# An earlier place for the first store's first transfer, coarser pieces in the first and the last tile, and the last store in two halves, in a SiLU-gate kernel

## The chip, the cores and the metric

One core of a Trainium2 chip. The metric is device time in microseconds (us) of the whole program, the median of several runs. The profile's span is some 2 us shorter than that time. All runs here are with a granted clock of 1.0.

## The reference

```python
def setup_inputs():
    batch, seq, dim = (32, 512, 2048)
    return {'x': np.random.randn(batch, seq, dim).astype(np.float32)}

def reference(x):
    half_dim = x.shape[-1] // 2
    x1, x2 = (x[..., :half_dim].copy(), x[..., half_dim:].copy())
    silu_x1 = x1 * (1 / (1 + np.exp(-x1)))
    return (silu_x1 * x2).astype(np.float32)
```

16,384 rows of 2,048 floats come in and rows of 1,024 go out: 134.2 MB read and 67.1 MB written, with one activation and one multiplication per output element.

## The kernel before

The rows are cut into 16 tiles. A tile gives each of the 128 partitions 8 rows, so it is an 8 MB load and a 4 MB store. Two input and two output buffers alternate. SyncE issues the loads. ScalarE (ACT) computes the SiLU and issues the stores. VectorE (DVE) multiplies in place.

```python
    K = 8
    KC_EDGE = 2
    OPENING = [                                   # (partitions, rows) of the first tile's four transfers
        (slice(0, None, 4), slice(0, 2)),         # 32 partitions x 2 rows: 256 KB
        (slice(0, None, 4), slice(2, None)),      # the same partitions, 6 rows: 768 KB
        (slice(2, None, 4), slice(None)),         # 32 partitions, 8 rows: 1 MB
        (slice(1, None, 2), slice(None)),         # 64 partitions, 8 rows: 2 MB
    ]
    # ... pools, views; silu() is one nc.scalar.activation, mul() one nc.vector.tensor_mul ...
    load(0)
    load(1)
    for i in range(n_tiles):
        xt = loaded.pop(i)
        ov = view(out_flat, i)
        ot = out_pool.tile([P, K, half], dt, name="ot")
        if i < n_tiles - 1:
            kc = KC_EDGE if i == 0 else K
            for c in range(0, K, kc):
                silu(ot, xt, c, c + kc)
                mul(ot, xt, c, c + kc)
            for ps, ks in OPENING if i == 0 else [(slice(None), slice(None))]:
                nc.scalar.dma_start(out=ov[ps, ks], in_=ot[ps, ks])
            if i + 2 < n_tiles:
                load(i + 2)
            continue
        cuts = list(range(0, K, KC_EDGE))         # the last tile: four pieces of 2 rows
        for n, c in enumerate(cuts + [None, None]):
            if c is not None:
                silu(ot, xt, c, c + KC_EDGE)
                mul(ot, xt, c, c + KC_EDGE)
            if n >= 2:
                b = cuts[n - 2]
                nc.scalar.dma_start(out=ov[:, b:b + KC_EDGE, :], in_=ot[:, b:b + KC_EDGE, :])
```

Of the kernel before, what the change touches and what calls it, by code (L numbers as in the profile page):

```python
# [1 line left out]

# [4 lines left out]


def issue_ahead_of_the_first_barrier(nc):




    head, body = nc.main_func.blocks[:2]
    load = next(ins for ins in body.instructions if type(ins).__name__ == "InstDMACopy")
    at = next(
        j for j, ins in enumerate(head.instructions)
        if ins.engine == load.engine and type(ins).__name__ == "InstDrain"
    )
    body.instructions = [ins for ins in body.instructions if ins.name != load.name]  # L20
    head.instructions = head.instructions[:at] + [load] + head.instructions[at:]


@with_exitstack
def kernel(
    ctx: ExitStack,
    tc: tile.TileContext,
    x: bass.AP,
    out: bass.AP,
):  # L30






    nc = tc.nc
    P = nc.NUM_PARTITIONS

    x_flat = x.flatten_outer_dims()  # L40
    out_flat = out.flatten_outer_dims()
    num_rows, in_cols = x_flat.shape
    half = in_cols // 2
    dt = x_flat.dtype

    K = 8
    KC_EDGE = 2
    OPENING = [
        (slice(0, None, 4), slice(0, 2)),
        (slice(0, None, 4), slice(2, None)),  # L50
        (slice(2, None, 4), slice(None)),
        (slice(1, None, 2), slice(None)),
    ]
    PLAN = [K] * (num_rows // (P * K))

    in_pool = ctx.enter_context(tc.tile_pool(name="in_pool", bufs=2))
    out_pool = ctx.enter_context(tc.tile_pool(name="out_pool", bufs=2))

    plan = []
    row = 0  # L60
    for k in PLAN:
        plan.append((row, k))
        row += P * k
    assert row == num_rows
    n_tiles = len(plan)

    def view(flat, i):
        row0, k = plan[i]
        return flat[row0:row0 + P * k].rearrange("(p k) d -> p k d", k=k)

    nc.at_finalize(issue_ahead_of_the_first_barrier)


    ctx.enter_context(tc.manual_schedule())

    loaded = {}

    def load(i):
        xt = in_pool.tile([P, K, in_cols], dt, name="xt")
        nc.sync.dma_start(out=xt[:, :plan[i][1], :], in_=view(x_flat, i))  # L80
        loaded[i] = xt

    def silu(ot, xt, c, ce):
        nc.scalar.activation(  # L84
            out=ot[:, c:ce, :],
            in_=xt[:, c:ce, :half],
            func=mybir.ActivationFunctionType.Silu,
        )

    def mul(ot, xt, c, ce):  # L90
        nc.vector.tensor_mul(  # L91
            out=ot[:, c:ce, :],
            in0=ot[:, c:ce, :],
            in1=xt[:, c:ce, half:],
# [6 lines that stand above are left out]
        ov = view(out_flat, i)  # L101
        ot = out_pool.tile([P, K, half], dt, name="ot")
        if i < n_tiles - 1:
            kc = KC_EDGE if i == 0 else K
            for c in range(0, K, kc):
                silu(ot, xt, c, c + kc)
                mul(ot, xt, c, c + kc)

            for ps, ks in OPENING if i == 0 else [(slice(None), slice(None))]:
                nc.scalar.dma_start(out=ov[ps, ks], in_=ot[ps, ks])  # L110
            if i + 2 < n_tiles:
                load(i + 2)
            continue

        cuts = list(range(0, K, KC_EDGE))
        for n, c in enumerate(cuts + [None, None]):
            if c is not None:
                silu(ot, xt, c, c + KC_EDGE)
                mul(ot, xt, c, c + KC_EDGE)
            if n >= 2:  # L120
                b = cuts[n - 2]
                nc.scalar.dma_start(out=ov[:, b:b + KC_EDGE, :], in_=ot[:, b:b + KC_EDGE, :])


# [1 line left out]
_INS = ['x']  # L126
_OUTS = [((32, 512, 1024), 'float32')]


# [23 lines left out]
```

## Time and profile before

| | before |
|---|---|
| median time (3 runs) | 470.49 us (470.48 to 470.6) |
| span | 468.5 us |
| ACT and DVE busy | 24% and 30% of the span |
| DMA | 430 GB/s over the span |

The page and its edges are read in the prediction. One more view: the windows of the kernel before. The columns are the stretch, its length, the busy time of DVE, ACT and POOL, the clock, the DMA share and GB/s.

```profile
36.00:44.00 8.00, 0.00 (x0) 0.00 (x0) 0.00 (x0) 1.00 1.21 492
26.00:48.00 22.00, 6.72 (x4) 6.85 (x3) 0.00 (x0) 1.00 1.03 429
```

A window books a packet whole where it starts, so the share can exceed 1 and 8 us are too short for a rate. The same windows of two kernels can still be held against each other.

A finer measure comes from the trace's packet records, and I call it **lost DMA time**: the length of a stretch, minus the time that the work done in it takes at the packets' undisturbed durations, as a mean over the 16 DMA engines. It counts both standing still and slow packets. The undisturbed pitch is 2.42 us for a 64 KB load packet and 1.21, 0.91, 0.61 and 0.31 us for store packets of 32, 24, 16 and 8 KB. For the kernel before it is 0.76 us from 26 to 48 us, and 0.0 to 0.02 us in every later stretch I tabulated. (Neighbouring packet records overlap by some 0.2% in the steady stretches. With their recorded durations taken as they are, the figure for a stretch of 22 us comes out about 0.05 us lower.) A "lane" below is one engine's string of packets. The records do not name the engine, so lanes are rebuilt from starts and ends.

### The profile page before, as it was taken

How to read it: one execution, taken by the hardware profiler on the slowest of the kernel's cores; microseconds unless marked ns; L12 is line 12 of the kernel's file. 1: busy time of each engine (PE TensorE's matmuls, PEld its weight loads, DVE VectorE, ACT ScalarE, POOL GpSimd, SP SyncE). 2: the span in 40 equal slices, each digit the busy share in tenths (PEclk: the TensorE clock that was granted, in tenths of full speed). 3: DMA queues.
4: the chain of work that ended last, by engine and by line, in shares of the span. 5: the costliest groups of instructions: out<-in, count | busy, mean ns of one | idle time of the engine just before them, and what ended most of it. 6: DMA issues, size and time to landing. Idle time of an engine off the chain costs nothing.

```text
span 468.5 us, 188 instructions
## 1 busy us (share of the span) xinstructions
DVE 139.5 (30%) x22; ACT 114.3 (24%) x23; POOL 0.2 (0%) x4
## 2 busy tenths in 40 slices
DVE  0070613407033070430704207052060510606151
ACT  1142306041060500505005050140601406023060
POOL 0000000000000000000000000000000000000000
DMA  9999999999999999999999999999999999999988
GB/s 431 392 453 380 448 425 425 492 403 403 448 476 420 403 448 425 470 403 428 422 492 403 403 448 487 408 403 448 425 470 403 425 425 492 403 403 448 481 371 357
DMA packets 5121, 201.34 MB, mean 430 GB/s; under 512 B 608, under 2 KB 608, under 8 KB 608
## 3 DMA queue, kind: packets, MB, share of 16 engines
q1 hardware_dynamic: 2304, 134.22, 66.4%
q10 hardware_dynamic: 2816, 67.11, 33.2%
q14 instruction: 1, 0.01, 0.0%
HBM read 134.22 MB, written 67.11 MB: 430 GB/s over the span
## 4 chain that ended last, share of the span: by engine, by line
DMA 72%; DVE 14%; ACT 11%; DVEq 0%; issue 0%; ACTq 0%
DMA xt<-in_x_dram 72%; DVE ot L91 14%; ACT ot L84 11%; DVEq L148 0%; ACTq L84 0%
## 5 line engine op out<-in xcount | busy, mean ns | idle before, releaser
L91 DVE TENSOR_TENSOR ot<-ot,xt 128x8192 f32<-128x8192 f32 (+1 forms) x22 | 139.5, 6362 | 319.6 <-ACT ot L84 319.6
L84 ACT ACTIVATE ot<-xt 128x8192 f32<-128x8192 f32 (+1 forms) x22 | 113.0, 5163 | 340.5 <-DMA xt<-in_x_dram 340.5
L84 ACT ACT_TABLE_LOAD x1 | 1.3, 1283 | 0.8 <-PEq L137 0.8
L137 POOL MEMSET const-bfloat16-1.0<- 128x1 bf16 x1 | 0.1, 101 | 0.0
L137 POOL MEMSET const-uint8-127<- 128x1 uint8 x1 | 0.1, 101 | 0.0
L137 POOL MEMSET const-float32-0.0<- 128x1 f32 x1 | 0.1, 98 | 0.2 <-issue 0.2
L137 POOL MEMSET const-float32-1.0<- 128x1 f32 x1 | 0.1, 98 | 0.0
## 6 DMA issues: line engine op xcount, KB each, us to landing
out_dram<-ot ACTq DMA_DIRECT2D x14, 4096.0 KB, 42.0
out_dram<-ot ACTq DMA_DIRECT2D x5, 1024.0 KB, 8.2
out_dram<-ot ACTq DMA_DIRECT2D x1, 2048.0 KB, 37.0
out_dram<-ot ACTq DMA_DIRECT2D x1, 768.0 KB, 11.7
xt<-in_x_dram SPq DMA_DIRECT2D x16, 42.1
out_dram<-ot ACTq DMA_DIRECT2D x1, 256.0 KB, 10.9
```

Source lines behind the costliest of these rows:

```text
L84: nc.scalar.activation(out=ot[:, c:ce, :], in_=xt[:, c:ce, :half], func=mybir.ActivationFunctionType.Silu,)
L91: nc.vector.tensor_mul(out=ot[:, c:ce, :], in0=ot[:, c:ce, :], in1=xt[:, c:ce, half:],)
L137: nc = _bacc.Bacc("TRN2", target_bir_lowering=False, num_devices=1)
```

## The change

The intent is to have the first store under way early, and to have fewer and larger pieces at the end. The first tile is computed in pieces of 2, 2 and 4 rows and the first transfer is issued after the second activation. The last tile is computed as 2, 2 and 4 rows and stored as two halves of 4.

```diff
-    KC_EDGE = 2
+    CHUNKS_FIRST = [2, 2, 4]
+    CHUNKS_LAST = [2, 2, 4]
+    KS = 4
@@ all tiles but the last
-            kc = KC_EDGE if i == 0 else K
-            for c in range(0, K, kc):
+            c = 0
+            chunks = CHUNKS_FIRST if i == 0 else [K]
+            parts = list(OPENING) if i == 0 else [(slice(None), slice(None))]
+            for n, kc in enumerate(chunks):
                 silu(ot, xt, c, c + kc)
+                if n == 1:
+                    ps, ks = parts.pop(0)
+                    nc.scalar.dma_start(out=ov[ps, ks], in_=ot[ps, ks])
                 mul(ot, xt, c, c + kc)
-            for ps, ks in OPENING if i == 0 else [(slice(None), slice(None))]:
+                c += kc
+            for ps, ks in parts:
                 nc.scalar.dma_start(out=ov[ps, ks], in_=ot[ps, ks])
@@ the last tile
-        cuts = list(range(0, K, KC_EDGE))
-        ... (four pieces, each stored two pieces later)
+        issued = None
+        c = 0
+        for kc in CHUNKS_LAST:
+            silu(ot, xt, c, c + kc)
+            if issued is None and c >= KS:
+                issued = slice(0, KS)
+                nc.scalar.dma_start(out=ov[:, issued], in_=ot[:, issued])
+            mul(ot, xt, c, c + kc)
+            c += kc
+        nc.scalar.dma_start(out=ov[:, KS:], in_=ot[:, KS:])
```

More of the change, by code (lines that the diff above doesn't have):

```diff
@@ L113 @@
             continue
-        cuts = list(range(0, K, KC_EDGE))
-        for n, c in enumerate(cuts + [None, None]):
-            if c is not None:
-                silu(ot, xt, c, c + KC_EDGE)
-                mul(ot, xt, c, c + KC_EDGE)
-            if n >= 2:
-                b = cuts[n - 2]
-                nc.scalar.dma_start(out=ov[:, b:b + KC_EDGE, :], in_=ot[:, b:b + KC_EDGE, :])
+        issued = None
[8 more added lines that the diff above has]
+        nc.scalar.dma_start(out=ov[:, KS:], in_=ot[:, KS:])
 _INS = ['x']
```

## The prediction

> **What bounds the kernel now.** I read the page first, then the windows (busy time and DMA by stretch), the timeline of the two edges, the waits, and last the trace's single DMA packet records, because the change touches only the first and the last tile.
>
> The page: compute is far from full, the DMA engines are full in all 40 slices but the last two, and those are at eight tenths.
>
> ```profile
> span 468.5 us, 188 instructions
> DVE 139.5 (30%) x22; ACT 114.3 (24%) x23; POOL 0.2 (0%) x4
> ...
> DMA  9999999999999999999999999999999999999988
> ...
> HBM read 134.22 MB, written 67.11 MB: 430 GB/s over the span
> ```
>
> The reader should see 201.3 MB in 468.5 us. Nothing in the change alters the bytes, so it can only win time in which DMA engines stand still or run slowly. The windows over five stretches and the tail say how much there is of that:
>
> ```profile
> 5.00:26.00 21.00, 2.18 (x1) 4.12 (x3) 0.00 (x0) 1.00 0.98 424
> 26.00:44.00 18.00, 6.72 (x4) 3.19 (x2) 0.00 (x0) 1.00 1.05 437
> 44.00:447.00 403.00, 121.69 (x14) 98.41 (x14) 0.00 (x0) 1.00 1.00 432
> 447.00:457.00 10.00, 6.80 (x4) 7.31 (x4) 0.00 (x0) 1.00 0.99 426
> 457.00:467.00 10.00, 2.10 (x1) 0.00 (x0) 0.00 (x0) 1.00 0.98 414
> ```
>
> The last two columns are the DMA share and GB/s. A window books a packet where it starts, so short windows are rough (1.05), but no stretch from 5 to 467 us has a hole worth a microsecond. The last row runs 4% under the middle one: there the packets are 8 KB instead of 32 KB.
>
> The packet records sharpen this. I spread each packet's bytes over its own duration and strung packets into 16 lanes, each beginning as another ends (the records do not name the engine, so the lanes are my reconstruction). From 1.0 us to 467.1 us the lanes have no gap to speak of: 0.07 us per lane in total. A 64 KB load packet takes 2.418 us, a 32 KB store packet 1.213 us, an 8 KB store packet 0.309 us. Slow packets occur in three places only, in us per lane: 0.73 at the very first load packets, 0.17 around 28 to 31 us, 0.57 in the load packet of 36.3 to 39.5 us (3.0 instead of 2.42 us in all lanes). Check: 16 tiles x 8 x 2.418 = 309.5; 15 store tiles x 8 x 1.213 = 145.6; the last tile 32 x 0.309 = 9.9; slow packets 1.5; sum 466.5 plus the start at 1.0 = 467.5, against a last packet ending at 467.13 (rounding and slight overlap). The remaining 1.4 us of the span is its end after the last packet.
>
> The edges in the timeline:
>
> ```profile
> 21.88 5.51 ACT L84 ACTIVATE ot<-xt 128x2048 f32<-128x2048 f32 x3 [19.83 <-DMA xt<-in_x_dram]
> 23.82 8.90 DVE L91 TENSOR_TENSOR ot<-ot,xt 128x2048 f32<-128x2048 f32 x4 [23.82 <-ACT ot L84]
> 26.15 0.55 ACTq L110 DMA_DIRECT2D out_dram<-ot  x1
> 27.30 1.89 ACT L84 ACTIVATE ot<-xt 128x2048 f32<-128x2048 f32 x1
> 32.75 1.78 ACTq L110 DMA_DIRECT2D out_dram<-ot  x3
> ...
> 450.20 8.90 DVE L91 TENSOR_TENSOR ot<-ot,xt 128x2048 f32<-128x2048 f32 x4 [15.17 <-ACT ot L84]
> 452.53 0.34 ACTq L122 DMA_DIRECT2D out_dram<-ot  x1
> 453.68 1.89 ACT L84 ACTIVATE ot<-xt 128x2048 f32<-128x2048 f32 x1
> 454.73 4.74 ACTq L122 DMA_DIRECT2D out_dram<-ot  x3
> ```
>
> Two things to see. The first transfer stands after all four activations in the code, yet goes out at 26.15 us, before the fourth activation starts: it waits for the first multiplication alone. And the chain of waits shows loads and compute alternating (72% DMA, 14% DVE, 11% ACT), but that chain is the longest dependency, not the limit: while ACT waits up to 22 us for a load, the engines carrying that load never stop.
>
> **What the Trainium skill says.** "Perfetto Trace Analysis", Roofline, puts a lone trn2 core's ceiling at its 16 DMA engines, about 435 GB/s; the spread packets run at 434 here, so it agrees. The same page, Per-instruction lifecycle, says that an activation's semaphore wait takes place in a queue behind the sequencer, which is then free for the next instruction; the 26.15 us issue agrees. "DMA: Bandwidth & Descriptors", Anatomy of one DMA, says that a DMA's wait happens on the issuing sequencer before dispatch: so an activation behind such an issue is held. Nothing here stands behind one, so this trace does not show it yet. The same page, Queues, rings and completion order, has each DMA engine take turns between queues by packets; the lanes alternate load, store, load, store wherever both queues have work.
>
> **The change part by part.**
>
> *First transfer issued between activations.* It needs the first multiplication, done at 26.1 us, so it is again issued at 26.15: gain 0. The third activation, now of 4 rows, stands behind it and cannot start at 25.5 but at about 26.15 + 0.55 = 26.7 us. Its length by interpolation: 1.892 us at 2048 elements and 7.029 at 8192 give 0.836 ns per element, so 4096 take 3.60 us, to 30.3. The 4-row multiplication, from 2.286 and 8.692 us in the same way, takes 4.42 us: 30.35 to 34.8, against 32.7 before. So the other three transfers and the third load go out at 34.8 instead of 32.75. Cost in compute 2.05 us; cost on the DMA path 0, since the second load occupies the lanes until about 43 us, and only then is the third load needed: 8 us of slack. Stores that come later let loads go first; the sum of packets is the same.
>
> *Last tile, 2, 2, 4 rows computed, stored as 4 and 4.* The last load's packets end at 447.6 us; then the lanes carry 8 packets of 32 KB of the store before it, to 456.8 to 457.3 us. That backlog covers the first issue, which moves from 452.53 to the end of the second multiplication, 454.73: 2.1 us to spare. The first half takes 8 packets of 16 KB. One 32 KB packet cut into four costs 4 x 0.309 - 1.213 = 0.023 us, 0.008 per extra packet, so 16 KB take 0.610 and the half 4.88 us, to 461.7 at the earliest. The 4-row activation starts at 448.26 + 2 x 1.81 = 451.9 and ends at 455.5; its multiplication ends at 459.9; the second issue comes at 459.95. From issue to first packet took 1.0 us for the first load, so its packets are ready at about 460.95: 0.75 us to spare. Then 4.88 us more. Gain: 32 x 0.309 - 16 x 0.610 = 9.89 - 9.76 = 0.13 us, and two semaphore packets of 0.01 us per lane less: 0.15 us.
>
> *Sum:* 470.49 + 0 - 0.15 = 470.34. I shade it to 470.3, for the small chance that the slow packets at 36 us get shorter.
>
> **The rivals.**
>
> *A: the slow packets at 28 to 39 us go.* They follow each opening issue by 2 to 5 us, and the pairs of a store and a load issued later in the run show none, so something of the opening causes them. If the new timing avoids them, up to 0.74 us goes: 469.6. Against it: the same four transfers with the same shapes, the first at the same moment.
>
> *B: the end gets a hole.* The second half is issued with 0.75 us to spare. If a store takes over 1.75 us from issue to first packet, the lanes stand still for the rest; with 2.5 us and a slow first packet as at the start (0.73) that is 0.75 + 0.73 = 1.5, so about 471.8. For it: the first transfer, issued at 26.15, showed no packet until 30.7 us. Against it: load packets had their turn there, 2.4 us each, and one seems to be committed ahead.
>
> *C: the later third load starves the lanes.* It would need to come after 41 us; at 34.8 I rule it out. If stores stood still too, 2 us: 472.4.
>
> *D: an earlier store start gives a real gain of several us.* It would need idle lanes during the opening. The windows show 424 and 437 GB/s there, so no.
>
> **Range and chances.** The step of -0.15 us is about the spread of the three runs (0.12). A adds -0.74 on one side, B some 1 us at perhaps one in six on the other. Predicted 470.3, range 469.5 to 471.3. Two per cent is 9.4 us, more than any rival gives, and all slow packets and holes together are 1.6 us: faster 0.005, same 0.985, slower 0.01.
>
> **What would show it right or wrong.** Right: first transfer at 26.1 to 26.2; a 4-row activation at 26.7 and of 3.6 us; the three others at about 34.8; third load too; end issues at 454.7 and 459.95; 16 KB packets without a hole near 461.7; last packet at about 467.0. Wrong: a transfer issued well before 26 (the wait was not what I take it for); a hole after 461 us (B); DMA windows from 26 to 44 us visibly emptier or fuller (A, C); or a middle of the run not at 432 GB/s, which no step here foresees.

## The result, and the profile after

| | before | after |
|---|---|---|
| median time (6 runs each) | 470.59 us (470.48 to 471.31) | 471.45 us (470.66 to 471.66) |
| span of the profiled run | 468.5 us | 469.8 us |

The ratio is 1.0013, with a 95% interval of 1.0001 to 1.0026. A ratio is the mean time of one kernel's fast runs over the mean of the other's, so it is not quite the ratio of the medians. The change is within 2%, a little on the slow side.

The page of the changed kernel, with the same lines as before:

```profile
span 469.8 us, 182 instructions
DVE 139.5 (30%) x20; ACT 114.2 (24%) x21; POOL 0.2 (0%) x4
...
DMA  9999999999999999999999999999999999999998
```

Busy times are the same and the DMA row is again full, so nothing on the page says where 1.3 us went. The timeline of its two edges, with start, duration, engine and what it waited for (ACTq and SPq are transfers issued by ScalarE and SyncE):

```profile
26.19 0.55 ACTq L114 DMA_DIRECT2D out_dram<-ot  x1
26.79 3.62 ACT L86 ACTIVATE ot<-xt 128x4096 f32<-128x4096 f32 x1 [1.15 <-DVE ot L93]
30.43 4.42 DVE L93 TENSOR_TENSOR ot<-ot,xt 128x4096 f32<-128x4096 f32 x1 [2.07 <-ACT ot L86]
34.89 1.80 ACTq L118 DMA_DIRECT2D out_dram<-ot  x3
45.38 7.03 ACT L86 ACTIVATE ot<-xt 128x8192 f32<-128x8192 f32 x1 [14.98 <-DMA xt<-in_x_dram]
...
449.69 7.22 ACT L86 ACTIVATE ot<-xt 128x2048 f32<-128x2048 f32 x3 [22.05 <-DMA out_dram<-ot]
...
456.15 0.34 ACTq L129 DMA_DIRECT2D out_dram<-ot  x1
456.93 4.42 DVE L93 TENSOR_TENSOR ot<-ot,xt 128x4096 f32<-128x4096 f32 x1 [0.81 <-ACT ot L86]
461.39 0.34 ACTq L132 DMA_DIRECT2D out_dram<-ot  x1
```

The first transfer still goes out at 26.2 us. Behind it the 4-row activation was held 1.15 us until the first multiplication was done. The three other transfers go out at 34.89 us. The second tile's activation starts at 45.38 us, against 44.34 before: its load landed 1.0 us later. The last tile begins at 449.69 us, against 448.26. So most of the loss is already there at 45 us, before any steady tile.

The windows of the changed kernel over the same stretches:

```profile
26.00:44.00 18.00, 6.79 (x3) 3.62 (x1) 0.00 (x0) 1.00 0.97 387
44.00:447.00 403.00, 121.69 (x14) 98.41 (x14) 0.00 (x0) 1.00 1.00 434
...
457.00:467.00 10.00, 4.36 (x1) 0.00 (x0) 0.00 (x0) 1.00 1.01 433
36.00:44.00 8.00, 0.00 (x0) 0.00 (x0) 0.00 (x0) 1.00 1.04 371
26.00:48.00 22.00, 6.79 (x3) 6.23 (x2) 0.00 (x0) 1.00 0.99 399
```

The middle of the run is as full as before (434 against 432). The last row (433 against 414) says little, because the window cuts the end at another place: e4, which has the same last tile at the old times, shows 403 GB/s in it. The opening is emptier: from 26 to 44 us 387 GB/s instead of 437, and from 26 to 48 us 399 instead of 429. Part of that gap is booking of packets at the window's edge; the sizes come from the packet records. Lost DMA time in that stretch is 1.46 us instead of 0.76, and this execution lost another 0.8 us between 48 and 446 us, of which 0.45 between 70 and 90 us.

### The profile page after: what moved, and what is told of

Its sections match the earlier page's. It is cut to its first block, busy times and chain, and to the rows that moved or that the text cites. A ratio compares the mean times of both kernels' runs of the same rounds, so it can differ in the third digit from the quotient of the medians.

```text
span 469.8 us, 182 instructions
## 1 busy us (share of the span) xinstructions
DVE 139.5 (30%) x20; ACT 114.2 (24%) x21; POOL 0.2 (0%) x4
## 4 chain that ended last, share of the span: by engine, by line
DMA 72%; DVE 14%; ACT 12%; issue 0%; ACTq 0%
DMA xt<-in_x_dram 36%; DMA out_dram<-ot 36%; DVE ot L93 14%; ACT ot L86 12%; ACTq L86 0%
## 5 line engine op out<-in xcount | busy, mean ns | idle before, releaser
L93 DVE TENSOR_TENSOR ot<-ot,xt 128x8192 f32<-128x8192 f32 (+2 forms) x20 | 139.5, 6985 | 321.8 <-ACT ot L86 321.8
L86 ACT ACTIVATE ot<-xt 128x8192 f32<-128x8192 f32 (+2 forms) x20 | 112.9, 5661 | 341.9 <-DMA xt<-in_x_dram 230.8
## 6 DMA issues: line engine op xcount, KB each, us to landing
out_dram<-ot ACTq DMA_DIRECT2D x14, 4096.0 KB, 42.2
```

Of the source, the lines that this page charges most:

```text
L86: nc.scalar.activation(out=ot[:, c:ce, :], in_=xt[:, c:ce, :half], func=mybir.ActivationFunctionType.Silu,)
L93: nc.vector.tensor_mul(out=ot[:, c:ce, :], in0=ot[:, c:ce, :], in1=xt[:, c:ce, half:],)
```

## The experiments

Twelve kernels ran, all correct. Those sent together share their runs of the kernel before, whose median is in the table; e9 to e11 reuse the eleven of e5 to e8 and add a single new one (471.04 us), so their small differences rest on the traces as well. "Later transfers" is when the first of the transfers after the small one went out in the profiled run. "Lanes in time" counts how many 24 KB packets (the first of the later transfers; two per lane in all) started before 41 us. In e12 more small packets run ahead of the 24 KB ones, so its 0 does not compare.

| run | median, us | before, us | ratio (95%) | later transfers, us | lanes in time | lost 26 to 48 us |
|---|---|---|---|---|---|---|
| e1_before_again | 470.66 | 470.53 | 1.0004 (0.9991 to 1.0016) | as before | 16 | 0.75 |
| e2_after_again | 471.16 | 470.53 | 1.0012 (1.0 to 1.0024) | 35.17 | 1 | 1.22 |
| e3_opening_only | 471.29 | 470.53 | 1.0022 (1.0004 to 1.004) | 34.72 | 11 | 1.13 |
| e4_last_only | 470.47 | 470.53 | 0.9996 (0.9983 to 1.0009) | as before | 16 | 0.76 |
| e5_hold_only | 470.58 | 470.66 | 0.9998 (0.9985 to 1.0011) | 33.15 | 16 | 0.78 |
| e6_chunks_only | 470.80 | 470.66 | 1.0003 (0.9991 to 1.0015) | 33.68 | 16 | 0.69 |
| e7_late_stores | 471.62 | 470.66 | 1.0038 (1.0011 to 1.0066) | 35.09 | 4 | 1.40 |
| e8_late_load | 470.61 | 470.66 | 0.9998 (0.9986 to 1.001) | 32.70 | 16 | 0.66 |
| e9_later_stores | 471.38 | 470.68 | 1.0016 (1.0002 to 1.0031) | 36.34 | 0 | 1.09 |
| e10_one_store | 470.60 | 470.68 | 0.9998 (0.9985 to 1.0011) | one, 32.72 | none of 24 KB | 1.08 |
| e11_late_end | 471.99 | 470.68 | 1.0029 (1.0014 to 1.0044) | 32.76 | 16 | 0.77 |
| e12_long_first | 470.44 | 470.66 | 0.9995 (0.9982 to 1.0009) | 34.77 | 0 | 0.65 |

The first profiles of the kernel before and of the changed kernel had 16 and 6 lanes in time, and lost 0.76 and 1.46 us.

### Is it real, and which end is it? e1 to e4

e1 and e2 are the two kernels unchanged. e3 has the new opening with the old last tile, and e4 the reverse:

```diff
 e3: CHUNKS_FIRST, parts and "if n == 1" as in the change; the last tile as before
 e4: the first tile as before; CHUNKS_LAST, KS and the last tile as in the change
```

> The kernel before, unchanged, for a second profile. All theories: ratio 1.000 within 0.001. Theory 1 (the later issue of three stores and the third load slows load packets at 36 to 42 us): slow packets at 26 to 44 us again 0.6 to 0.8 us per lane. Theory 2 (the slow packets are chance stalls of an execution): another sum, anywhere from 0 to 1.5 us.

> The changed kernel, unchanged, for a second profile. Theory 1: slow packets at 26 to 44 us again about 1.4 us per lane, ratio about 1.0013. Theory 2: another sum, not clearly above that of the kernel before, and stalls elsewhere in the run at other times than in the first profile (77 to 80 us).

> The new opening with the old last tile. Theory 1: all of the loss and none of the gain: ratio about 1.0016, some 471.4 us, slow packets at 26 to 44 us about 1.4 us per lane. Theory 2: within 0.3 us of the kernel before. Theory 3 (the two 2 MB pieces at the end cost the time): equal to the kernel before.

> The old opening with the new last tile. Theory 1: the gain alone, 0.15 us: ratio about 0.9997, some 470.4 us. Theory 2: within 0.3 us of the kernel before. Theory 3: about 471.4 us, ratio 1.0015, with a hole or slow packets after 457 us.

The old opening lost 0.76, 0.75 and 0.76 us in three profiles, so its slow packets are no accident. The new opening lost 1.46, 1.22 and 1.13 us: always more, and not constant. The stall at 77 to 80 us of the first profile did not come back in e2, so it is no fixed part of the change (e7 lost 0.4 us again between 70 and 90 us). e3 has all of the loss (median 471.29; one of its six runs took 474.0 and lifts the ratio) and e4 none. e4's window is that of the kernel before, word for word in its last two columns, and its second half goes out just where the prediction put it:

```profile
26.00:48.00 22.00, 6.67 (x4) 6.80 (x3) 0.00 (x0) 1.00 1.03 429
```

```profile
454.73 0.34 ACTq L123 DMA_DIRECT2D out_dram<-ot  x1
455.51 4.42 DVE L93 TENSOR_TENSOR ot<-ot,xt 128x4096 f32<-128x4096 f32 x1 [0.81 <-ACT ot L86]
459.97 0.34 ACTq L126 DMA_DIRECT2D out_dram<-ot  x1
```

Its last packet ended at 467.03 us, against 467.13 before. The loss is the opening's.

### What in the opening: e5 to e8

The new opening does three things: an issue holds up ACT, the three later transfers come later, and the third load comes later. Four kernels take these apart.

```diff
 e5 (e3, four pieces of 2 rows)
-    CHUNKS_FIRST = [2, 2, 4]
+    CHUNKS_FIRST = [2, 2, 2, 2]
 e6 (the kernel before, pieces of 2, 2, 4; all transfers after them; the lines that count c are left out)
-            for c in range(0, K, kc):
+            for kc in [2, 2, 4] if i == 0 else [K]:
 e7 (the kernel before; after the first tile's pieces)
+            if i == 0:
+                nc.vector.tensor_copy(out=ot[:, 4:8, :], in_=ot[:, 4:8, :])
 e8 (the same place)
+            if i == 0:
+                nc.vector.tensor_copy(out=xt[:, 4:8, :half], in_=xt[:, 4:8, :half])
```

The copies change no value. In e7 only the stores must wait for the copy, in e8 only the load that reuses the buffer.

> First tile still in four pieces of 2 rows, but the first transfer between the activations. By the durations on record the other three transfers and the third load go out at about 33.2 us (before 32.75, new opening 34.9). Lost DMA time at 26 to 48 us was 0.76 us per lane with the old opening (3 profiles) and 1.13 to 1.46 with the new one. Theory 1a (it is the lateness of the three transfers or of the load): about 0.8 to 0.9, time within 0.2 us of before. Theory 1d (it is the holding up of the activation engine by the issue, whatever the lateness): 1.1 to 1.4, some 0.6 us slower.

> First tile in pieces of 2, 2, 4 rows, all four transfers after them in the code. The first transfer still goes out at about 26.2, the other three and the third load at about 33.6 us. Theory 1a: lost time between the two openings, 0.8 to 1.1; 1d: 0.76, as before.

> The kernel before with a copy of the last 4 rows of the first output tile onto themselves, so that the three transfers wait for it and the third load does not: load at 32.75 us, transfers at about 35. Theory 1b (late stores reach some lanes a turn later than others, and that costs): lost time 1.1 to 1.5 us per lane at 26 to 48 us, some 0.5 us slower. Theory 1c (the late load does it): 0.76 and equal.

> The kernel before with a copy of half of the last 4 rows of the first input tile onto themselves, so that the third load waits for it and the transfers do not: transfers at 32.75 us, load at about 35. Theory 1b: lost time 0.76 us per lane and equal to before. Theory 1c: 1.1 to 1.5, some 0.5 us slower.

The timeline of e7, then its window:

```profile
32.76 0.33 SPq L80 DMA_DIRECT2D xt<-in_x_dram  x1
32.76 2.29 DVE L109 COPY ot<-ot 128x4096 f32<-128x4096 f32 x1
35.09 1.78 ACTq L112 DMA_DIRECT2D out_dram<-ot  x3
```

```profile
26.00:48.00 22.00, 9.02 (x5) 5.87 (x3) 0.00 (x0) 1.00 0.99 402
```

And those of e8:

```profile
32.59 2.29 DVE L109 COPY xt<-xt 128x4096 f32<-128x4096 f32 x1
32.70 1.77 ACTq L112 DMA_DIRECT2D out_dram<-ot  x3
34.95 0.33 SPq L80 DMA_DIRECT2D xt<-in_x_dram  x1
```

```profile
26.00:48.00 22.00, 8.87 (x5) 6.92 (x3) 0.00 (x0) 1.00 1.02 429
```

The two kernels differ in which of the two waits, and the answer is one-sided. Late stores bring 402 GB/s, 1.40 us lost and +0.96 us in the medians. A late load brings 429 GB/s, 0.66 us lost and no change. e5 shows that holding up ACT costs nothing, and e6 that the 4-row piece costs nothing as long as the transfers go out by 33.7 us. Theory 1a expected 0.8 to 1.1 us lost in e6 and that was a miss: 0.9 us of lateness cost nothing (0.69 us). So the late stores of theory 1b are the cause, against 1c and 1d, and the loss sets in between 33.7 and 34.7 us. Whether lanes that miss a turn are what costs, as 1b has it, is tested next.

e7 also went on losing after the opening: its profiled run, 476.36 us, was by far its slowest (the other five took 471.46 to 472.36). It lost another 2.6 us between 48 and 446 us, and its lanes ended between 469.2 and 473.0 us, where those of the kernel before end within 0.6 us of each other.

### Turns, or lateness, or an empty queue: e9, e10, e12

The packet records show each lane taking load and store packets in turn. In the kernel before, all 16 lanes take the first 24 KB packet at 39.3 to 39.7 us, after the load packet that started at 36.3 to 36.7 us. Transfers issued at 34.72 us or later reach only some of the lanes in time for that turn, and the column "lanes in time" falls with the time of issue: 16 at 33.7, 11 at 34.72, 6 at 34.89, 4 at 35.09, 1 at 35.17. Does the damage lie in that split? e9 is so late that all lanes miss alike. e10 has no small first transfer at all.

```diff
 e9 (e7 with a longer copy)
-                nc.vector.tensor_copy(out=ot[:, 4:8, :], in_=ot[:, 4:8, :])
+                nc.vector.tensor_copy(out=ot[:, 2:8, :], in_=ot[:, 2:8, :])
 e10 (the kernel before)
-    OPENING = [ ... four transfers ... ]
+    OPENING = [(slice(None), slice(None))]
```

> As e7_late_stores, but the copy covers 6 rows, so that the three transfers go out at about 36.2 us; the third load again at 32.75. Theory 1b as a matter of turns (transfers issued near 35 us reach some lanes before and some after the choice that each makes at about 36.4 us for its next packet): now all lanes miss that choice alike, so they stay together, lost time at 26 to 48 us falls back towards 0.8, and the time towards 470.7 us. Rival 1e (the later the stores, the more is lost): over 1.4 us lost, 472 us or more.

> The kernel before with the first tile's output in one transfer of 4 MB, issued at about 32.75 us, instead of four. If the 0.57 us of slow load packets at 36 to 39 us in the kernel before belongs to the small first transfers, it goes, and the time is about 469.9; if it belongs to the store queue taking up work at all, lost time stays near 0.6 to 0.8 and the time equal. If the four transfers are what brings the lanes into step, lost time rises and the run is slower than before by 0.5 us or more.

e9 fell between its two expectations. No lane was in time and all stayed together, yet it lost 1.09 us and ran 0.70 us behind the medians of before. So being split is not the whole cost, and lateness is not simply proportional either: e7, issued 1.25 us earlier, lost more.

The packets say what is common. The load packet that runs just ahead of a lane's first 24 KB packet took 2.42 us plus a median of 0.57 us in the kernel before, e1, e4, e5, e6 and e8 (0.54 to 0.58), but plus 1.03 us in e9. In e10 the load packet ahead of the first store packet took 1.07 us more as a mean of all lanes, and e10 lost 1.08 us. In its time e10 shows nothing of this (470.60 us, equal to before; its last packet ended 0.25 us later), so its expected 0.5 us was a miss, and 0.3 us of lost time is near what the timing can't resolve.

What e9 and e10 share is a turn without a store packet: the long load packet followed straight on another load packet. In e9 the two 8 KB packets that each lane has of the first transfer were used up by 34.4 us, and the 4-byte packet that closes the transfer ran at 36.3 to 36.9 us, one load packet before the long one; in the kernel before it ran at 36.3 to 36.7 us, right before the slow one. The store queue had thus run dry, although it was not empty of work any more when the long packet started (38.7 to 39.3 us): e9's later transfers had been issued at 36.34 us. In the kernel before, the later transfers had been issued (32.75 us) before the queue ran out.

One thing in the traces speaks against the lane's own queue as the whole cause. In the changed kernel's two profiles and in e7, a load packet that started between 38.5 and 40.9 us ran long in all 16 lanes, by medians of 1.17, 1.13 and 1.19 us. That includes the 6, 1 and 4 lanes that were in time. There it came after the first 24 KB packet (it started at 40.1 to 40.8 us) and still took 1.14 to 1.71 us more. So something that all lanes share may set the 1.1 us; no run tests that.

My reading was the dry queue. That gave theory 1f, and e12 for it: the changed kernel, with a first transfer that gives each lane four small packets instead of two.

```diff
     OPENING = [
-        (slice(0, None, 4), slice(0, 2)),
-        (slice(0, None, 4), slice(2, None)),
-        (slice(2, None, 4), slice(None)),
+        (slice(0, None, 2), slice(0, 2)),
+        (slice(0, None, 2), slice(2, None)),
         (slice(1, None, 2), slice(None)),
```

> The changed kernel with another split of the first store: first transfer 64 partitions x 2 rows (4 packets of 8 KB per lane instead of 2), then their other 6 rows, then the other 64 partitions. The two later transfers again go out at about 34.9 us. Theory 1f (the loss comes when the store queue has run dry before the later transfers are taken: two small packets are used up by 34.2 us, four last to about 39): the queue isn't dry, slow packets at 36 to 44 us fall to 0.2 us per lane or less, lost time at 26 to 48 us to 0.5 or less, and the run is as fast as the kernel before or up to 0.5 us faster. Theories 1b and 1e (lateness or turns alone): lost time 1.1 us or more and about 471.3 us.

The timeline of e12, then its window:

```profile
26.66 3.62 ACT L85 ACTIVATE ot<-xt 128x4096 f32<-128x4096 f32 x1 [1.15 <-DVE ot L92]
...
34.77 1.15 ACTq L117 DMA_DIRECT2D out_dram<-ot  x2
43.17 7.03 ACT L85 ACTIVATE ot<-xt 128x8192 f32<-128x8192 f32 x1 [12.89 <-DMA xt<-in_x_dram]
```

```profile
26.00:48.00 22.00, 6.66 (x3) 8.45 (x2) 0.00 (x0) 1.00 1.01 426
```

ACT is held as in the changed kernel and the later transfers go out as late, at 34.77 us. Yet 0.65 us is lost instead of 1.13 to 1.46, and the median is 470.44 us against 470.66 for the kernel before. All five runs (470.36 to 470.50) lie below all nine of the kernel before (470.52 and up), though the interval of the ratio holds 1. So theory 1f held on the time, but not on its sharper number: I expected slow packets of 0.2 us at most and they came to 0.55, in the load packet ahead of the first 24 KB packet, now at 42.3 us, in all lanes. With more small packets in the store queue the excess over 0.57 us is gone, and the 0.57 us itself is not. It also shows that missing the turn at 39 us costs nothing by itself: no lane took a 24 KB packet before 42.2 us.

What stays open: why a load packet runs longer around a lane's first large store packets, and why by 1.0 to 1.2 us in some kernels, in lanes that were in time too. And e12 changes two things against the changed kernel, the length of the small packets' row and the number of transfers (three for four), so it supports the dry queue as the cause without isolating it; the changed kernel itself was not run again beside it. In e9 and e12 there are also small losses, 0.4 us in all from 90 to 446 us, which the kernel before has not, and which no run explains.

### The margin at the end: e11

```diff
 e11 (e4, ahead of the second half's issue)
+        nc.vector.tensor_copy(out=ot[:, 4:8, :], in_=ot[:, 4:8, :])
         nc.scalar.dma_start(out=ov[:, KS:], in_=ot[:, KS:])
```

> The old opening with the new last tile, and a copy of 4 rows onto themselves before the second half goes out: issue at about 462.3 us instead of 459.97, while the lanes finish the first half at 461.8 to 462.4. It measures what the prediction's rival B feared. With 1.0 us from issue to first packet the lanes stand still for 0.9 to 1.5 us: 471.5 to 472.2 us. With 2.5 us: 473 us or more. If the second half were not at the edge at all: equal.

The timeline of e11, then its windows:

```profile
460.06 2.29 DVE L126 COPY ot<-ot 128x4096 f32<-128x4096 f32 x1
462.39 0.34 ACTq L127 DMA_DIRECT2D out_dram<-ot  x1
```

```profile
460.00:464.00 4.00, 2.32 (x2) 0.00 (x0) 0.00 (x0) 1.00 0.70 299
```

The lanes finished the first half at 461.7 to 462.3 us and took the second half's first packet at 463.23 us, 0.84 us after its issue began. They stood still for 1.4 us (lost time from 460 to 464 us), and the time rose by 1.31 us to 471.99, inside the expected 471.5 to 472.2. No packet after that hole was slow by more than 0.05 us.

The same hole, by itself, occurred in e2: a single lane, the one that was in time, came out of the opening a turn behind the others, the last load landed late, the second half was issued at 461.71 us and its first packets came at 462.56, while most lanes had been ready since 462.3. That execution took 472.04 us. In e4 the second half was issued 1.7 us before the first half ended.

## Why the prediction was right or wrong

The direction of the sum was wrong by a small amount. Predicted were 470.3 us and 469.5 to 471.3. The measured median is 471.45, 0.15 us above that range; 470.49 us times the ratio of 1.0013 is 471.1, inside it. That it comes so near is luck: the upper end was drawn for rival B, a hole at the end, and the loss came from the opening. One of the prediction's own signs of being wrong showed, the window from 26 to 44 us (387 GB/s against 437), and the last packet ended at 468.48 us instead of about 467.0. That the change stays within 2% was right, for the reason given: the DMA engines are full, and there is little to win or lose.

- **First transfer, gain 0:** right. It went out at 26.19 us (predicted 26.15), because it waits for the first multiplication in either place.
- **The hold-up of ACT:** right in every term. The 4-row activation at 26.79 for 3.62 us (predicted 26.7 and 3.60), the multiplication 4.42 us as predicted, the three transfers and the load at 34.89 (predicted 34.8).
- **"Cost on the DMA path 0 ... Stores that come later let loads go first; the sum of packets is the same":** this is the step that failed. The argument for the load held (e8: 34.95 us, no loss). For the stores it took packet durations as fixed. They are not: with the transfers 2 us later, one load packet in each of the 16 lanes took some 1.1 to 1.2 us more (medians of 1.17, 1.13 and 1.19 us in the changed kernel's two profiles and e7), where the kernel before has one slowed by 0.57 us. In e3 two load packets per lane were slowed by less, 0.97 us in sum. Mis-sized term: 0, measured 0.4 to 0.7 us of lost DMA time in three profiles, plus what some executions lose afterwards. That late stores do this is shown (e7 against e8); why the load packets then run longer stays open.
- **The last tile, gain 0.15 us:** right within what can be measured. e4 is 0.06 us below in the medians, its last packet 0.10 us earlier; issues at 454.73 and 459.97 (predicted 454.73 and 459.95), 16 KB packets of 0.611 us (predicted 0.610). In the changed kernel everything at the end is 1.4 us later: 1.0 us from the opening, the rest from the later stalls of that execution. The prediction's remark that its last window runs 4% lower because of 8 KB packets was wrong: with 16 KB packets, e4 shows 403 GB/s there, still less than 414.
- **Rival A** looked at the right kind of packet, the slow loads at 28 to 39 us, and weighed only that they might go. The weak link was "the same four transfers with the same shapes, the first at the same moment": it is the other three whose moment mattered.
- **Rival B:** its estimate of 1.0 us from issue to first packet measured 0.84 (e11), so the hole did not come of itself; but it came in one execution (e2), through the opening.
- **Rivals C and D** were rightly ruled out: e8 for the load; and the first transfer in its new place (e5) wins nothing.

## What to carry to other kernels

When every DMA engine is full, moving an issue can still cost, through the packets' durations: look at single packets where a second queue joins in, not only at bytes and gaps. Before making the pieces ahead of a store coarser, ask how late the next transfers will come. Here keeping the pieces small was safe (e5), and so was a longer early transfer, whose packets keep the store queue busy until then (e12, 470.44 us). And a DMA issue in an engine's program order holds what stands behind it until its own wait is over, here 1.15 us of ACT.

## What the Trainium skill lacked or had wrong

- "DMA: Bandwidth & Descriptors", Queues, rings and completion order: it has the turns between queues, and the lanes agree. It lacks that a load packet can run longer just before a lane takes up large store packets: by 0.54 to 0.58 us of 2.42 in the kernel before and five others, by 1.03 and 1.07 us where the store queue had run dry (e9, e10; the reason is not isolated); and that transfers issued near a turn reach only a part of the engines in it (16, 11, 6, 4, 1, 0 for issues at 33.68, 34.72, 34.89, 35.09, 35.17, 36.34 us).
- The same page, Latency and other measured facts: it gives about 600 ns to the first byte of a DMA from SyncE or ScalarE, without saying from where it is counted. Here an idle store queue's first packet started 0.84 us after the issue began, which is 0.50 us after the 0.34 us issue ended (e11).
